# Two matmuls of one weight block joined into one of 512 columns, in the feed-forwards of a two-block transformer kernel

## The chip, the cores and the metric

The kernel runs on one core of a Trainium2 chip. Its time is device microseconds from start to end of one execution. A run of the profiler also gives a span, from the first to the last instruction. The engines are named as in the profile: PE is the matrix engine and PEld its weight loads, DVE is VectorE, ACT is ScalarE, POOL is GpSimd, SP issues the transfers.

## The reference

One sequence of 256 tokens with 1024 features goes through two stacks of two layers each. The parts that matter here are the feed-forwards:

```
# first stack, i = 0, 1 (w_ff_in: 1024 x 4096, w_ff_out: 4096 x 1024)
u = rms_norm(h, g_ffn_pre[i])
f = square(relu(u @ w_ff_in[i])) @ w_ff_out[i]
h = h + rms_norm(f, g_ffn_post[i])

# second stack (w_up: 1024 x 5632, w_down: 2816 x 1024); a = h @ w_up
g, u = a[..., :2816], a[..., 2816:]
acc = conv_b + gp[:, 0:T] * conv_w[0] + gp[:, 1:T+1] * conv_w[1] + gp[:, 2:T+2] * conv_w[2]
return (silu(acc) * u) @ w_down        # gp: g padded by one token at both ends
```

The second stack has a main stream of 256 tokens, which goes through the conv feed-forward in both layers, and a context stream of 256 tokens, which goes through it in the first layer only. The rest is attention of four kinds (stick-breaking, dilated, latent with pooling, grouped), gates, norms, and a conditioning product that gives scales and shifts. Everything is float32.

## The kernel before

**Exact sums of two parts.** A float32 number is held as a high part, rounded to the matrix engine's float32r, and a low part, the rest. A product of two such numbers takes three matmuls (`mm3`, L193 to L196): high by high, high by low, low by high. Weights come from memory as float32 blocks of 128 x 1024 into a ring of four buffers (`ws`); ACT casts each block to its high part (L182) and DVE subtracts (L183), in halves of 512 columns, into rings of four high and four low blocks (`wh`, `wl`). The ring buffer is free again when both halves are subtracted.

**Activations.** `Feat` holds the normalised activations with features on partitions, as chunks of 128 features x 256 tokens, each with a high and a low part. A norm (`norm_one`, L241) runs for each half of the tokens: the row's scale from ACT, DVE and POOL, then for every group of chunks one DVE operation that normalises (L251, or L253 with a shift), transposes on PE into a PSUM bank (L230), a copy of the high part by ACT (L199) and a subtraction by DVE (L200). A group is four chunks (512 columns), or two where `paired` is set; with `paired` the high and low parts of a pair of chunks are in one tile. Main activations come from a pool of eight 4 KB tiles (`m4`), the context's from one of eleven (`c4`).

**First feed-forward** (`ffn1`, L605). Sixteen groups of 256 hidden features per layer. For a group, `up` takes two blocks of weights; for each of two chunks of 128 hidden features the weight block is the stationary side, and 256 tokens of activations move past it, eight blocks of the 1024 inputs, three matmuls each. Both chunks fill one PSUM bank of 512 columns. Then ReLU (ACT, L622), square (DVE, L623), split. `down` multiplies the hidden features (stationary) by 512 columns of the second matrix, into two accumulators. The loop issues `up` of the next group, a piece of filler work, then `down` of this one.

**Conv feed-forward** (`ffn2`, L1088; `up_chunk`, L1072; `conv_chunk`, L1057). For each of 22 chunks the gate half and the up half are each eight blocks of three matmuls, and fill the two halves of one bank. `conv_chunk` reads them there: a tap with bias on ACT (L1062), two more taps on DVE (L1064, L1066), SiLU (ACT, L1068), a product (DVE, L1069), a split. The context stream runs the same two functions from `ctx_gen`, in groups of four chunks.

**Order.** The engines' programs are laid out by a scheduler at build time from the order of the code and the dependencies, so an engine's order can differ from the code's; at run time each engine goes through its own list in order. The code itself mixes streams: `fill` steps generators of filler work (the context stream, or the conditioning product, whose step loads two 512 KB blocks and multiplies them at L465) by a table of credits, `FILL`, between pieces of the main stream.

**Banks.** PSUM has two accumulators of two banks, two banks for the main stream (`mm`), and two for fillers (`fx`, the conditioning product among them).

Of the kernel before, what the change touches and what calls it, by code (L numbers as in the profile page):

```python
# [9 lines left out]
F32 = mybir.dt.float32  # L10
# [10 lines left out]
T = 256  # L21
# [80 lines left out]
def two_block_kernel(ctx: ExitStack, tc: tile.TileContext, a: dict, out: bass.AP, dbg=None):  # L102
# [20 lines left out]
    def mm1():  # L123
        return mmp.tile([128, 512], F32, tag="mm", name="mm")
# [42 lines left out]
    # ---------------------------------------------------------------- helpers  # L167
# [25 lines left out]
    def mm3(o, lh, ll, rh, rl, start, stop):  # L193
        pe.matmul(o, lh, rh, start=start, stop=False)  # L194
        pe.matmul(o, lh, rl, start=False, stop=False)  # L195
        pe.matmul(o, ll, rh, start=False, stop=stop)  # L196

# [60 lines left out]
    class Feat:  # L258
        """Feature-major activations as an exact sum of two float32r parts, by chunks of 128 features."""

        def __init__(self, alloc, n, name, paired=False):
            self.H, self.L, self.groups = [], [], []
            per = 2 if paired else 4
            for c0 in range(0, n, per):
                cn = min(per, n - c0)
                if paired:
                    t = alloc([128, 2, cn, T], F32R, name)
                    th, tl = t[:, 0], t[:, 1]
                else:
                    th = alloc([128, cn, T], F32R, name + "h")  # L270
                    tl = alloc([128, cn, T], F32R, name + "l")
                self.groups.append((th, tl))
                for c in range(cn):
                    self.H.append(th[:, c, :])
                    self.L.append(tl[:, c, :])

# [9 lines left out]
    def tok_blocks(y, us, blocks, first, last):  # L286
        # y[tt] += us[k]^T @ blocks[k], token tile by token tile
        for tt in range(2):
            ts = slice(tt * 128, (tt + 1) * 128)
            for k, ((uh, ul), (bh, bl)) in enumerate(zip(us, blocks)):  # L290
                for nh in range(2):
                    s = slice(nh * 512, nh * 512 + 512)
                    mm3(y[tt][:, s], uh[:, ts], ul[:, ts], bh[:, 0, s], bl[:, 0, s],
                        first and k == 0, last and k == len(us) - 1)
# [13 lines left out]
    # ---------------------------------------------------------------- fillers  # L308
# [40 lines left out]
    def until_dense(n):  # L349
        # bring the context stream to products that wait for nothing  # L350
        clean("mod")
        while queues["ctx"] and dense[0] < n:
            fill_step("ctx")
        credit["ctx"] = 0.0
# [7 lines left out]
    # ------------------------------------------------------------ small setup  # L362
# [17 lines left out]
    def setup_cond():  # L380
        # silu of the two conditionings as columns
        cr = tmp((128, 128))
        nc.sync.dma_start(out=cr[0:8, :], in_=a["c_2"].rearrange("b (k p) -> (b k) p", p=128))
        nc.sync.dma_start(out=cr[8:16, :], in_=a["c_ctx_2"].rearrange("(k p) -> k p", p=128))
        ps = fx1()
        pe.transpose(ps[:, 0:16], cr[0:16, :], ident[0:16, 0:16])
        gp.memset(cst, 0.0)
        act.activation(out=cst[:, :, 0:2], in_=ps[:, 0:16].rearrange("p (r k) -> p k r", r=2), func=AF.Silu)

    def setup_later():  # L390
        nc.sync.dma_start(out=misc, in_=ca[:, C_IF:C_END])
        # rope of the first block
# [26 lines left out]
    def setup_last():  # L419
# [6 lines left out]
        # per-feature columns: conv taps and biases, pool scales  # L426
# [21 lines left out]
    # ------------------------------------------------------- conditioning GEMV  # L448
# [27 lines left out]
    # ------------------------------------------------------------ first block  # L476
# [128 lines left out]
    def ffn1(i, u, before_end):  # L605
        w1, w2 = a["w_ff_in"][i], a["w_ff_out"][i]
        G = FF1 // 256
        with tc.tile_pool(name="ff", bufs=2) as p:
# [3 lines left out]
            def up(g):  # L612
                blocks = [wblock(w1, b * 4, 4, g * 256, 256) for b in range(2)]
                ps = mm1()
                for c in range(2):
                    for kc in range(8):
                        bh, bl = blocks[kc // 4]
                        s = slice(c * 128, (c + 1) * 128)
                        mm3(ps[:, c * 256:(c + 1) * 256], bh[:, kc % 4, s], bl[:, kc % 4, s],
                            u.H[kc], u.L[kc], kc == 0, kc == 7)  # L620
                r = p.tile([128, 512], F32, tag="r", name="r")
                act.activation(out=r, in_=ps, func=AF.Relu)  # L622
                vec.tensor_mul(out=r, in0=r, in1=r)  # L623
                hh = p.tile([128, 2, T], F32R, tag="hh", name="hh")
                hl = p.tile([128, 2, T], F32R, tag="hl", name="hl")
                put_split(hh, hl, r.rearrange("p (c t) -> p c t", c=2))
                hT[g] = (hh, hl)
# [190 lines left out]
    # ----------------------------------------------------------- second block  # L818
# [49 lines left out]
    def mla_gen(u, rope, p, alloc, bank, pair, score_pair, res, prev):  # L868
        # queries, keys, values and pooled features of one stream; attends prev keys and its own
# [57 lines left out]
        # keys come out by features: pairs of heads, then the shared rotated part under each head  # L927
# [32 lines left out]
        # pooled features  # L960
# [27 lines left out]
        # attention  # L988
# [9 lines left out]
    def soft_heads(nh, nk, q, k, v, dv, scale, dst, p, al, bank, score_pair):  # L998
        # softmax attention over nk groups of 256 keys; scores of one head run ahead of the transposes of the last
# [57 lines left out]
    def conv_chunk(i, f, ps, p, hh, hl):  # L1057
        # ps: [128, 512] with the gate half and the up half of feature chunk f
        g, u = ps[:, 0:256], ps[:, 256:512]
        cw = cvw[i]  # L1060
        t = p.tile([128, T], F32, tag="cv", name="cv", bufs=2)
        act.activation(out=t, in_=g, func=AF.Identity, scale=cw[:, NCH + f:NCH + f + 1],  # L1062
                       bias=cw[:, 3 * NCH + f:3 * NCH + f + 1])
        vec.scalar_tensor_tensor(out=t[:, 1:T], in0=g[:, 0:T - 1], scalar=cw[:, f:f + 1], in1=t[:, 1:T],  # L1064
                                 op0=ALU.mult, op1=ALU.add)
        vec.scalar_tensor_tensor(out=t[:, 0:T - 1], in0=g[:, 1:T], scalar=cw[:, 2 * NCH + f:2 * NCH + f + 1],  # L1066
                                 in1=t[:, 0:T - 1], op0=ALU.mult, op1=ALU.add)
        act.activation(out=t, in_=t, func=AF.Silu)  # L1068
        vec.tensor_mul(out=t, in0=u, in1=t)  # L1069
        put_split(hh, hl, t)  # L1070

    def up_chunk(i, f, u, bank):  # L1072
        w = a["ffn_w_up_2"][i].rearrange("k (r n) -> k r n", r=2)
        ps = bank()
# [5 lines left out]
        for r in range(2):  # L1080
            for kc in range(8):
                bh, bl = blocks[kc // 4]
                o = (kc % 4) * 256 + r * 128
                mm3(ps[:, r * 256:(r + 1) * 256], bh[:, o:o + 128], bl[:, o:o + 128], u.H[kc], u.L[kc],
                    kc == 0, kc == 7)
# [49 lines left out]
    def ctx_norm(k, i, m):  # L1135
        g, sft = mod_row(i, 1, m + 1), mod_row(i, 1, m)
        u = Feat(c4, KC, "uc")
# [71 lines left out]
    def gain_tables(p, grow):  # L1209
        # per token and feature: gain x cos, and the gain of the partner feature x (-sin, +sin)  # L1210
# [18 lines left out]
    def gain_rope(x, ps, nh, tt, tables):  # L1229
        # x = rotated gain * ps for token-major heads of 128  # L1230
# [112 lines left out]
    # ------------------------------------------------------------------ order  # L1343
    def main_norm(g, shift=None):
        u = Feat(m4, KC, "u")
# [105 lines left out]
```

## Time and profile before

| | |
|---|---|
| median of three runs | 1740.43 us (1735.95, 1740.43, 1746.13) |
| profiled execution: span | 1732.4 us, 28608 instructions |
| profiled execution: its whole time | not recorded; the timed runs lie 3.6 to 13.7 us above the span |
| mean granted TensorE clock | 0.993 |
| transfers | 337.72 MB, mean 195 GB/s |

A line of the profile names the source line, the engine, the operation, what it writes and reads, and the count; "busy" is the time in which the engine had an instruction in flight, and the mean duration of a matmul includes its pipeline, so that the durations of matmuls overlap. "Idle ... <-" names what ended an engine's idle time. A stretch is given in microseconds from the start of the span. The stick-breaking attention and its projections fill the span up to 195 us, the first feed-forward runs from about 205 to 413, the gate and the dilated attention follow, the second layer's feed-forward runs from 705 to 893, the latent attention from about 950 to 1165, then come the main stream's conv feed-forward (1180 to 1405), the grouped attention, and the last conv feed-forward (1534 to 1717).

### The profile page before, as it was taken

What the parts mean: (1) busy time and instruction counts of PE and PEld (TensorE: products, weight loads), DVE (VectorE), ACT (ScalarE), POOL (GpSimd) and SP (SyncE); (2) the same over time, 40 slices, a digit from 0 to 9 for tenths busy, and PEclk for the clock granted to TensorE, in tenths of its full rate; (3) what the DMA queues carried; (4) which work ended last, traced back from release to release, by engine and by line L of the source; (5) the groups of instructions that cost most, each with busy time, mean ns of one, the idle gap of its engine ahead of it and who ended that gap; (6) DMA issues with size and microseconds to landing.
All of it is one profiled execution on the core that took longest, in us unless ns stands there. A gap on an engine that the chain in (4) does not pass through costs nothing.

```text
span 1732.4 us, 28608 instructions
## 1 busy us (share of the span) xinstructions
PE 1662.8 (96%) x10465; PEld 1428.1 (82%) x10468; DVE 1106.5 (64%) x2153; ACT 925.7 (53%) x1853; POOL 42.3 (2%) x65
## 2 busy tenths in 40 slices
PE   7998999999999999999999999999999999989997
PEld 6767888987887667888888988988999987779997
DVE  4437644557775446744667777767666887766665
ACT  5536544556654435544556556755555555545554
POOL 0000000000000000000000000000000000000000
PEclk9999999999999999999999999999999999989999
DMA  7777577654666666676756655446666765246663
GB/s 237 259 260 250 178 243 260 215 182 142 212 193 211 206 193 206 198 255 231 226 173 191 201 164 166 131 146 202 188 204 188 244 197 169 67 153 186 186 187 99
DMA packets 301073, 337.72 MB, mean 195 GB/s; under 512 B 18400, under 2 KB 246180, under 8 KB 300932
## 3 DMA queue, kind: packets, MB, share of 16 engines
q1 hardware_dynamic: 300932, 335.89, 61.7%
q8 instruction: 82, 1.34, 0.3%
q14 instruction: 59, 0.48, 0.1%
HBM read 332.57 MB, written 3.24 MB: 194 GB/s over the span
## 4 chain that ended last, share of the span: by engine, by line
PE 45%; DMA 5%; DVE 5%; ACT 2%; issue 1%; POOL 1%; SPq 0%; POOLq 0%; ACTq 0%; DVEq 0%
PE mm L196 6%; PE mm L194 6%; PE mm L195 6%; PE acc L195 5%; PE acc L196 5%; PE acc L194 5%; PE fx L196 3%; PE fx L194 3%; PE fx L195 3%; DMA ws<-in_w_ff_out 2%; DMA ws<-in_w_ff_in 2%; DVE wl L183 2%; PE acc L1007 1%; ACT wh L182 1%; PE mm L1033 1%
## 5 line engine op out<-in xcount | busy, mean ns | idle before, releaser
L183 DVE TENSOR_TENSOR wl<-ws,wh 128x512 fp32r<-128x512 f32 x1004 | 638.9, 668 | 402.7 <-ACT wh L182 391.4
L182 ACT CAST wh<-ws 128x512 fp32r<-128x512 f32 x1004 | 567.4, 603 | 510.3 <-PE mm L195 125.2
L194 PE MATMUL mm<-uh,wh 128*128 128x256 f32 x1344 | 382.8, 285 | 2.9 <-ACT wh L182 2.2
L196 PE MATMUL mm<-uh,wl 128*128 128x256 f32 x1344 | 382.0, 284 | 0.9 <-DVE wl L183 0.9
L195 PE MATMUL mm<-ul,wh 128*128 128x256 f32 x1344 | 381.6, 284 | 0.0
L194 PEld LDWEIGHTS mm<-uh,wh 128*128 128x128 f32 x1344 | 258.7, 192 | 8.7 <-ACT wh L182 3.0
L195 PEld LDWEIGHTS mm<-ul,wh 128*128 128x128 f32 x1344 | 258.8, 193 | 3.0 <-issue 0.4
L196 PEld LDWEIGHTS mm<-uh,wl 128*128 128x128 f32 x1344 | 258.7, 192 | 2.1 <-DVE wl L183 1.9
L194 PE MATMUL acc<-wh,hh 128*128 128x512 f32 x432 | 172.1, 398 | 0.0
L196 PE MATMUL acc<-wh,hl 128*128 128x512 f32 x432 | 169.6, 393 | 0.0
L195 PE MATMUL acc<-wl,hh 128*128 128x512 f32 x432 | 169.2, 392 | 0.0
L194 PEld LDWEIGHTS acc<-wh,hh 128*128 128x128 f32 x432 | 81.3, 188 | 28.7 <-ACT wh L182 5.9
L196 PE MATMUL fx<-uch,wl 128*128 128x256 f32 x352 | 100.6, 286 | 2.9 <-DVE wl L183 2.8
L194 PE MATMUL fx<-uch,wh 128*128 128x256 f32 x352 | 101.0, 287 | 1.7 <-DVE fsum L1191 1.7
L195 PE MATMUL fx<-ucl,wh 128*128 128x256 f32 x352 | 100.4, 285 | 0.0
L196 PEld LDWEIGHTS acc<-wh,hl 128*128 128x128 f32 x432 | 81.2, 188 | 18.3 <-issue 0.8
L195 PEld LDWEIGHTS acc<-wl,hh 128*128 128x128 f32 x432 | 81.4, 188 | 14.8 <-issue 0.4
L194 PE MATMUL mm<-wh,uh 128*128 128x384 f32 (+1 forms) x256 | 86.0, 337 | 2.1 <-ACT wh L182 1.6
L195 PE MATMUL mm<-wl,uh 128*128 128x384 f32 (+1 forms) x256 | 83.3, 325 | 0.6 <-DVE wl L183 0.6
L196 PE MATMUL mm<-wh,ul 128*128 128x384 f32 (+1 forms) x256 | 82.9, 324 | 0.0
L216 POOL TENSOR_TENSOR s<-s,neghalf 128x1 f32<-128x1 f32 (+2 forms) x52 | 38.7, 744 | 1556.5 <-DVE s L214 1556.5
L465 PE MATMUL fx<-ws,cst 128*32 128x512 f32 x384 | 65.0, 607 | 6.7 <-DMA ws<-in_w_mod 5.7
(397 smaller groups left out, 2658.9 us busy)
## 6 DMA issues: line engine op xcount, KB each, us to landing
ws<-in_ffn_w_up SPq DMA_DIRECT2D x528, 128.0 KB
ws<-in_w_mod SPq DMA_DIRECT2D x96, 512.0 KB
ws<-in_ffn_w_down SPq DMA_DIRECT2D x66, 512.0 KB
ws<-in_w_ff_in SPq DMA_DIRECT2D x64, 512.0 KB
ws<-in_w_ff_out SPq DMA_DIRECT2D x64, 512.0 KB
ws<-in_w_in_dil SPq DMA_DIRECT2D x96, 192.0 KB
ws<-in_w_in_sb SPq DMA_DIRECT2D x24, 512.0 KB
row<-mod SPq DMA_DIRECT2D x19, 512.0 KB
```

Of the source, the lines that this page charges most:

```text
L182: act.copy(out=h[:, s], in_=st[:, s])
L183: vec.tensor_sub(out=l[:, s], in0=st[:, s], in1=f32(h[:, s]))
L194: pe.matmul(o, lh, rh, start=start, stop=False)
L195: pe.matmul(o, lh, rl, start=False, stop=False)
L196: pe.matmul(o, ll, rh, start=False, stop=stop)
L216: gp.tensor_tensor(out=r, in0=v, in1=neghalf.to_broadcast([128, w]), op=ALU.pow)
L465: pe.matmul(ps[32 * q:32 * q + 32, :], cst[:, kc, :], st[:, q2 * 512:(q2 + 1) * 512], start=kc == 0, stop=kc == 7)
L1007: pe.matmul(sc[qt][:, n * 256:(n + 1) * 256], q(hd, qt), k(hd, n), start=True, stop=True)
L1033: pe.matmul(o, v(hd, n, kt), PTs[hd][:, 2 * n + kt, :], start=n == 0 and kt == 0, stop=n == nk - 1 and kt == 1)
```

## The change

`mm_wide` replaces `mm3` in the first matrices of the feed-forwards: the high part of the weight block is loaded once and meets 512 columns, the 256 tokens' high parts and then their low parts; the block's low part meets the high parts alone, in the first 256 columns. A bank so holds one chunk, with two partial sums. `add_halves` copies the second half out with ACT, into a tile that shares the one buffer of the norms' scratch (`junk`), and adds with DVE. To have high and low parts in one tile, the activations of all main norms and of the context's norms are `paired`.

In `ffn1` each chunk of 128 has its own bank, addition, ReLU and square (one DVE operation) and split. In the conv feed-forward the gate half and the up half each have their own bank; the gate is summed into a tile of the pool `xd` (two buffers, shared with the conditioning product's bias and a context tile), the up half into the same tile after the taps have read it.

```diff
+    def mm_wide(o, wh, wl, u, k, start, stop):
+
+        pe.matmul(o, wh, u.HL[k], start=start, stop=False)
+        pe.matmul(o[:, 0:256], wl, u.H[k], start=False, stop=stop)
+
+    def add_halves(out, ps):
+        b = tmpp.tile([128, 512], F32, tag="junk", name="hb", bufs=1)[:, 0:256]
+        act.copy(out=b, in_=ps[:, 256:512])
+        vec.tensor_tensor(out=out, in0=ps[:, 0:256], in1=b, op=ALU.add)
...
+                if paired:
+                    self.HL.append(t[:, :, c, :])
...
             def up(g):
                 blocks = [wblock(w1, b * 4, 4, g * 256, 256) for b in range(2)]
-                ps = mm1()
+                hh = p.tile([128, 2, T], F32R, tag="hh", name="hh")
+                hl = p.tile([128, 2, T], F32R, tag="hl", name="hl")
                 for c in range(2):
+                    ps = mm1()
                     for kc in range(8):
                         bh, bl = blocks[kc // 4]
                         s = slice(c * 128, (c + 1) * 128)
-                        mm3(ps[:, c * 256:(c + 1) * 256], bh[:, kc % 4, s], bl[:, kc % 4, s],
-                            u.H[kc], u.L[kc], kc == 0, kc == 7)
-                r = p.tile([128, 512], F32, tag="r", name="r")
-                act.activation(out=r, in_=ps, func=AF.Relu)
-                vec.tensor_mul(out=r, in0=r, in1=r)
-                hh = p.tile([128, 2, T], F32R, tag="hh", name="hh")
-                hl = p.tile([128, 2, T], F32R, tag="hl", name="hl")
-                put_split(hh, hl, r.rearrange("p (c t) -> p c t", c=2))
+                        mm_wide(ps, bh[:, kc % 4, s], bl[:, kc % 4, s], u, kc, kc == 0, kc == 7)
+                    r = p.tile([128, 256], F32, tag="r", name="r")
+                    add_halves(r, ps)
+                    vec.scalar_tensor_tensor(out=r, in0=r, scalar=0.0, in1=r, op0=ALU.max, op1=ALU.mult)
+                    put_split(hh[:, c, :], hl[:, c, :], r)
...
     def conv_chunk(i, f, ps, p, hh, hl):
-        # ps: [128, 512] with the gate half and the up half of feature chunk f
-        g, u = ps[:, 0:256], ps[:, 256:512]
         cw = cvw[i]
+        g = fillp.tile([128, 512], F32, tag="xd", name="cg", bufs=2)[:, 0:T]
+        add_halves(g, ps[0])
...
+        add_halves(g, ps[1])
         act.activation(out=t, in_=t, func=AF.Silu)
-        vec.tensor_mul(out=t, in0=u, in1=t)
+        vec.tensor_mul(out=t, in0=g, in1=t)
...
     def up_chunk(i, f, u, bank):
         w = a["ffn_w_up_2"][i].rearrange("k (r n) -> k r n", r=2)
-        ps = bank()
+        ps = [bank(), bank()]
...
-                mm3(ps[:, r * 256:(r + 1) * 256], bh[:, o:o + 128], bl[:, o:o + 128], u.H[kc], u.L[kc],
-                    kc == 0, kc == 7)
+                mm_wide(ps[r], bh[:, o:o + 128], bl[:, o:o + 128], u, kc, kc == 0, kc == 7)
...
     def ctx_norm(k, i, m):
-        u = Feat(c4, KC, "uc")
+        u = Feat(c4, KC, "uc", paired=True)
...
     def main_norm(g, shift=None):
-        u = Feat(m4, KC, "u")
+        u = Feat(m4, KC, "u", paired=True)
```

## Rows read from the trace of the kernel before

**Rows 1.** The page's first part: busy us, share of the span, instructions.
```profile
PE 1662.8 (96%) x10465; PEld 1428.1 (82%) x10468; DVE 1106.5 (64%) x2153; ACT 925.7 (53%) x1853; POOL 42.3 (2%) x65
```

**Rows 2.** The page's fourth part: shares of the chain that ended last, by engine.
```profile
PE 45%; DMA 5%; DVE 5%; ACT 2%; issue 1%; POOL 1%; SPq 0%; POOLq 0%; ACTq 0%; DVEq 0%
```

**Rows 3.** Stretches: busy us (count) by engine, then PE clock, DMA share, GB/s.
```profile
734.00:824.00 90.00, 88.62 (x569) 73.55 (x561) 43.07 (x68) 38.07 (x69) 0.00 (x0) 1.00 0.70 238
836.00:892.00 56.00, 56.00 (x362) 51.20 (x361) 32.17 (x51) 28.13 (x51) 0.00 (x0) 1.00 0.68 215
...
1185.00:1360.00 175.00, 175.00 (x1223) 164.34 (x1223) 120.64 (x218) 93.48 (x186) 0.00 (x0) 1.00 0.67 202
1540.00:1715.00 175.00, 175.00 (x1250) 165.45 (x1249) 112.80 (x209) 94.97 (x189) 0.00 (x0) 1.00 0.58 175
```

**Rows 4.** Groups on PE, 734 to 824: count, busy us, mean ns, idle.
```profile
L465 PE MATMUL fx<-ws,cst 128*32 128x512 f32 x64 | 8.5, 605 | 0.0
```

**Rows 5.** The chain of waits in order of time: start us, us, what.
```profile
723.11 4.52 DMA ws<-in_w_ff_out
727.73 0.63 ACT wh L182
728.39 1.31 DVE wl L183 x2
729.71 3.88 DMA ws<-in_w_ff_in
```

**Rows 6.** Timeline of PE, 836.4 to 847.8: start us, us, instruction, count.
```profile
836.47 0.40 PE L194 MATMUL acc<-wh,hh 128*128 128x512 f32 x1
...
841.71 0.39 PE L196 MATMUL acc<-wh,hl 128*128 128x512 f32 x1
841.93 0.28 PE L194 MATMUL mm<-uh,wh 128*128 128x256 f32 x1
...
847.69 0.40 PE L194 MATMUL acc<-wh,hh 128*128 128x512 f32 x1
```

**Rows 7.** Groups by line and shape, whole run: the blocks' first products.
```profile
L194 PE MATMUL mm<-uh,wh 128*128 128x256 f32 x1344 | 382.8, 285 | 2.9 <-ACT wh L182 2.2 <-DVE ul L200 0.5
...
L194 PE MATMUL fx<-uch,wh 128*128 128x256 f32 x352 | 101.0, 287 | 1.7 <-DVE fsum L1191 1.7
```

**Rows 8.** The same view, operations like the added and removed ones.
```profile
L200 DVE TENSOR_TENSOR hl<-r,hh 128x512 fp32r<-128x512 f32 x32 | 22.0, 687 | 0.8
L623 DVE TENSOR_TENSOR r<-r 128x512 f32<-128x512 f32 x32 | 21.9, 685 | 3.8 <-ACT r L622 3.7
...
L622 ACT ACTIVATE r<-mm 128x512 f32<-128x512 f32 x32 | 19.0, 593 | 4.9 <-PE mm L196 4.9
...
L1064 DVE SCALAR_TENSOR_TENSOR cv<-mm,cvw,cv 128x255 f32<-128x255 f32 x44 | 21.0, 477 | 0.6 <-ACT cv L1062 0.4
...
L1069 DVE TENSOR_TENSOR cv<-mm,cv 128x256 f32<-128x256 f32 x44 | 18.7, 424 | 21.2 <-ACT cv L1068 21.2
...
L200 DVE TENSOR_TENSOR hl<-cv,hh 128x256 fp32r<-128x256 f32 x44 | 18.4, 419 | 2.8 <-ACT hh L199 2.8
...
L717 ACT COPY tok<-mm 128x256 f32<-128x256 f32 x24 | 8.9, 371 | 8.1 <-PE mm L196 8.0
```

**Rows 9.** Waits from 734 to 824: total us, times, longest us.
```profile
PEld acc L194 <- ACT r L622: 2.5, 3, 0.8
```

**Rows 10.** Timeline of the norm at 1527, its end, with the first product.
```profile
1531.31 0.74 DVE L253 SCALAR_TENSOR_TENSOR t<-t,s,row 128x512 f32<-128x512 f32 x1
...
1531.97 0.68 DVE L200 TENSOR_TENSOR ul<-mm,uh 128x512 fp32r<-128x512 f32 x1
...
1532.57 0.68 DVE L183 TENSOR_TENSOR wl<-ws,wh 128x512 fp32r<-128x512 f32 x1
...
1533.97 0.58 PE L194 MATMUL mm<-uh,wh 128*128 128x256 f32 x1
```

**Rows 11.** What PE waited for before the flips (L230): total us, times.
```profile
  DVE t L251: 20.3, 7
```

More of the change, by code (lines that the diff above doesn't have):

```diff
@@ L261, in __init__ @@
         def __init__(self, alloc, n, name, paired=False):
-            self.H, self.L, self.groups = [], [], []
+            self.H, self.L, self.HL, self.groups = [], [], [], []
             per = 2 if paired else 4
```

## The prediction

> **What bounds the kernel now.** I read the busy shares first: TensorE's matmuls cover 96% of the 1732.4 us span, VectorE 64%, ScalarE 53% [rows 1]. The reader should see one engine that is nearly full and two that are not. The chain of waits says the same less strongly: PE has 45% of it, DMA and DVE 5% each [rows 2]. Next, stretch by stretch. From 1185 to 1360 and from 1540 to 1715 (the two conv feed-forwards of the main stream) PE is busy for all 175 us of 175, and also for all 56 us of 836 to 892, the end of the second layer's first feed-forward [rows 3]. There every matmul nanosecond removed is a nanosecond of the span, as long as the other engines keep up: VectorE stands at 120.6 and 112.8 us of 175. The stretch 734 to 824 differs: PE idles 1.4 of 90 us, and the transfers run at 238 GB/s. There eight loop turns each take a step of the conditioning product as well, with two more 512 KB loads (64 records of L465: a step has four products, and each is recorded twice) [rows 4], and the chain of waits runs through DMA, cast, subtraction and the next DMA, round and round, with no matmul in it [rows 5]: the ring of four weight buffers is as late as PE.
>
> **What a matmul costs.** A matmul's duration column is a pipelined latency and can't be summed; I take start to start. Forty-eight 256-column matmuls follow each other from 841.93 to 847.69: 120.0 ns each. The twenty-four 512-column ones before them run from 836.47 to 841.93: 227.5 ns each [rows 6]. So 512 columns cost less than twice 256: 240 against 227.5, a fixed part of some 12.5 ns per matmul. That difference is what the change sells.
>
> The Trainium skill (TensorE: Matmul & The Clock Gate, "Back-to-back issue gap") puts the gap at the columns over 2.4 GHz plus about 2.5 ns. By that rule each fusion saves 2.5 ns, 3.9 us over 1568 of them. The rows contradict it: 120.0 and 227.5 ns leave 12.5 ns at stake, not 2.5.
>
> **Removed.** Every block had three 256-column matmuls, 360 ns; now one of 512 and one of 256, 347.5 ns. The blocks: 32 groups x 16 = 512 in the first block's feed-forwards, 44 chunks x 16 = 704 in the main conv feed-forwards, 22 x 16 = 352 in the context stream's. The first two and 128 blocks of the stick-breaking projections are the 1344 of "mm", the last the 352 of "fx" [rows 7]. 1568 x 12.5 ns = 19.6 us, 0.2 us for each group or chunk. The new moving operand is two pieces of 256 columns, 512 columns apart; no row has such an operand. I take 227.5 ns; the bounds are 215 (twice the 107.5 ns by which 256 more columns lengthen a matmul, with no fixed part) and 240 (no gain).
>
> What of it reaches the end: the 44 main chunks run where PE is full, 8.8 us; the 16 groups without a conditioning step too, 3.2 us. Of the 16 groups beside a conditioning step (eight per layer: the row of L465 over 215 to 310 reads the same) 3.2 us are at stake, and the buffer ring takes most: I count 1.0, bounds 0 and 3.2. The context chunks, 4.4 us, are fillers, some in stretches where PE has gaps: I count 3.0. Together 16.0 us.
>
> **Added on ScalarE and VectorE.** A copy of the second half out of PSUM is like the 256-wide copy of L717, 371 ns; the addition is like L1069, 424 ns (one operand in PSUM, one not) [rows 8]. Per conv chunk: two copies 0.74 us, two additions 0.85 us. Per group of the first feed-forward: ReLU (593) becomes two copies (742); the 512-wide square (685) and split subtraction (687) become two additions (848), two fused max-multiply (by L1064, 477 each: 954) and two subtractions (2 x 419): VectorE +1.27 us. For 1540 to 1715 that makes some 22 x 0.85 = 19 us more, DVE 131 of about 171; in 1185 to 1360, with some 17 main and four context chunks, 139 of about 171. PE hides it: both still have 20% idle. If that cover went, a microsecond of delay per turn would cost 76 us over 32 groups and 44 chunks.
> The chains behind the products do not get longer: the gate half now has its own bank and is read while the up half multiplies, some 2.8 us earlier (eight blocks of 347.5 ns), and in the first feed-forward the last half is 256 wide. In 734 to 824 PE's weight loads waited 2.5 us for that ReLU [rows 9]; some of this may go.
>
> **Added in the banks.** A chunk now holds both banks of its pool. The first bank is freed while the second half multiplies, the second about 371 + 424 ns after the end, in the main loops under a down product of 12 x 227.5 = 2.7 us. Where two chunks stand back to back (each loop's first two, the context groups of four) up to half a microsecond shows: 1.5 us in all, bounds 0 and 6.
>
> **Moved: the norms.** The activations of all ten main norms and three context norms now come in pairs of chunks, so each token half makes four flips of two transposes, not two of four. In the norm at 1527 the normalising operations (L253) and the subtractions follow each other on VectorE 0.66 and 0.60 us apart, and PE waits for them between the transposes [rows 10]; over the run such waits for L251 alone hold back PE for 20.3 us in 7 places [rows 11]. At 256 columns I take the starts 0.40 and 0.345 us apart (477 and 419 ns, less the 75 ns by which a start comes before the end). Eight of each cost 5.96 us against 4 x 1.27 = 5.1: +0.86. The last flip has two transposes fewer: -0.22. That is +0.64 us for a norm that VectorE paces; context matmuls stand between the transposes of several, so I count 0.5 each: 5 us for ten. Bounds -2 (only the shorter tail shows) and +17 (each flip waits for its bank: 1.7 us a norm). SP's queue issues the same DMAs in the same order; POOL gets nothing new.
>
> **Sum.** -16.0 + 5.0 + 1.5 = -9.5 us: the profiled span would go from 1732.4 to about 1723. The whole time of that execution isn't shown; the median of the three runs, 1740.4, lies 8.0 us above its span, and I keep that distance: 1731 us.
>
> **Rivals.**
> Full gain: the norms' longer chain hides behind context matmuls and the shorter ReLU tail gives back what the buffer ring takes. For it: fillers stand at most norms. Against: the waits of rows 11. Time: 1740.4 - 18 = about 1722.
> Eaten up: the flips are paced by their two banks, +1.2 us per norm, and the context chunks' gain is lost in gaps: -13 + 12 + 2 = +1, 1741. Against it: the shorter transposes and copies.
> Slower, from ScalarE's and VectorE's order: their queues run in order, and each half now puts a copy that waits for PE, and an addition behind it, ahead of casts and subtractions of weights already landed. In 734 to 824 the ring has no slack, so 2 x 0.4 us per group over 32 groups would cost 25 us against 16 gained, plus the norms: +14, 1754. It decides once a cast is held up longer than PE's stock of converted blocks lasts (four buffers). For it: the ring's chain passes through a cast and a subtraction at every turn [rows 5]. Against: half of the new work comes earlier than the old.
> The change does not do what it says: the two-piece operand costs two matmuls' 240 ns. Then only the norms and banks stay: 5.0 + 1.5 = +6.5, 1747. For it: no row has such an operand. Against: the 227.5 ns of every 512-column row. The Trainium skill's rule above (same page and section) leads nearly as far, to -3.9 + 6.5, about 1743; the rows of 120.0 and 227.5 ns speak against it.
>
> **How the numbers follow.** Forecast 0.48, full gain 0.17, eaten up 0.16, slower 0.13, no cheaper matmul 0.06. Half a per cent, 8.7 us, is about what a measurement of this kernel can tell from no change; the three runs alone spread over 10 us. The forecast lies at that line: a little over half of it counts as faster. Faster 0.27 + 0.17 = 0.44; same 0.21 + 0.16 + 0.03, half of the last, = 0.40; slower 0.13 + 0.03 = 0.16. The forecast's own range is 1724 to 1738. For 8 in 10 I go down into the full gain, 1718, and up past "eaten up" and the 240 ns matmul to 1749.
>
> **What would show it.** Right: in 1540 to 1715's stage a turn of 8.5 us becomes 8.3, with a 512-column "mm" starting 227 ns before the next matmul; PE full there still. In the turns with a conditioning step nearly the same period as before, the chain still through DMA. In the norms sixteen transposes in eight pairs, and from the first normalising operation to the first product some 0.6 us more. Wrong: a pitch of 240 ns; waits of PE for casts or subtractions in the conv stages; PE held up by the added copy or addition, for a bank; or norms no longer than before, and the time near 1722.

## The result, and the profile after

| | before | after |
|---|---|---|
| median (range, runs) | 1742.59 us (1735.95 to 1746.13, 4) | 1760.99 us (1757.69 to 1771.23, 4) |
| ratio after / before | | 1.012 [1.008, 1.016] |
| profiled execution: span | 1732.4 us | 1756.2 us |
| profiled execution: whole time | not recorded | 1758.04 us |
| mean granted TensorE clock | 0.993 | 0.983 |

The kernel is 1.2% slower; the forecast was 1731 us, with a range of 1718 to 1749. The whole time of an execution turns out to lie 1.8 us above its span, not 8: the profiled execution of before then took 1734 us, less than any of the four runs. So the spans' difference of 23.8 us is some 5 us larger than the medians' of 18.4, and where sizes matter below I use ratios and not spans.

The page's first part after: busy us, share of the span, instructions.
```profile
PE 1666.0 (95%) x8896; PEld 1346.0 (77%) x8900; DVE 1194.1 (68%) x2517; ACT 981.8 (56%) x2100; POOL 41.4 (2%) x65
```
Against [rows 1], 1569 matmuls are gone, yet PE is busy 3.2 us longer and idle 20.6 us longer (1756.2 less 1666.0 is 90.2, before it was 69.6). Both halves need an answer.

The stretches that answer to [rows 3], after: busy us (count) by engine, PE clock, DMA share, GB/s.
```profile
742.00:832.00 90.00, 89.33 (x463) 68.99 (x461) 51.55 (x101) 40.45 (x84) 0.00 (x0) 1.00 0.70 238
845.00:901.00 56.00, 56.00 (x285) 47.44 (x284) 39.34 (x75) 31.71 (x66) 0.00 (x0) 1.00 0.70 214
1200.00:1375.00 175.00, 175.00 (x915) 148.20 (x914) 133.75 (x259) 107.75 (x228) 0.00 (x0) 1.00 0.65 194
1565.00:1735.00 170.00, 170.00 (x899) 145.10 (x898) 125.13 (x247) 106.85 (x226) 0.00 (x0) 1.00 0.61 180
```
Inside the loops PE is full as forecast, VectorE and ScalarE have room for the copies and additions, and from 742 to 832 transfers run at 238 GB/s as before. The loss is elsewhere. PE's longest waits after, and what it waited for (us, times, longest):
```profile
PE mm L240 <- DVE t L261: 17.1, 4, 9.9
PE mm L240 <- DVE t L263: 12.3, 2, 6.1
...
PE mm L200 <- DVE cg L206: 4.4, 1, 4.4
```
The same view of before has these (L230, L251 and L253 there are L240, L261 and L263 here):
```profile
PE mm L230 <- DVE t L251: 10.1, 4, 8.8
PE mm L230 <- DVE t L253: 7.4, 3, 6.4
```
So 11.9 us more go into waiting for a norm's first operation, and 4.4 us into one conv chunk's addition. To see why, one norm is followed in both kernels. The timeline of before, PE with one of ACT's squares, at the norm of the second layer's first feed-forward (start us, us, instruction, idle before and releaser):
```profile
693.83 0.39 PE L196 MATMUL acc<-wh,o 128*128 128x512 f32 x1
694.05 0.28 PE L194 MATMUL fx<-uch,wh 128*128 128x256 f32 x1
...
696.36 1.06 ACT L222 ACTIVATE junk<-h 128x1024 bf16<-128x1024 f32 x1
...
700.05 0.28 PE L196 MATMUL fx<-uch,wl 128*128 128x256 f32 x1
700.66 0.66 PE L230 MATMUL mm<-ident,t 128*128 128x128 f32 x4 [0.34 <-DVE t L251]
```
After, the same place, with ACT's squares and the copy:
```profile
687.41 0.28 PE L201 MATMUL fx<-uc,wl 128*128 128x256 f32 x1
...
701.91 0.39 PE L196 MATMUL acc<-wh,o 128*128 128x512 f32 x1
702.40 1.02 ACT L232 ACTIVATE junk<-acc 128x1024 bf16<-128x1024 f32 x1 [0.28 <-PE acc L196]
704.44 1.05 ACT L232 ACTIVATE junk<-h 128x1024 bf16<-128x1024 f32 x1
706.93 1.06 ACT L232 ACTIVATE junk<-h 128x1024 bf16<-128x1024 f32 x1 [1.34 <-DVE s L224]
708.11 0.37 ACT L205 COPY hb<-fx 128x256 f32<-128x256 f32 x1
708.48 0.93 PE L240 MATMUL mm<-ident,t 128*128 128x128 f32 x3 [6.18 <-DVE t L261]
...
713.49 0.41 DVE L206 TENSOR_TENSOR cg<-fx,hb 128x256 f32<-128x256 f32 x1
714.04 0.77 PE L200 MATMUL fx<-uc,wh 128*128 128x512 f32 x1
```
Before, six microseconds of a context chunk's products run from 694.05 to 700.05, while ACT squares the main stream for its norm (L222); PE has a gap of 0.34 us. After, a context chunk's sixteen blocks are done at 687.7 and hold both `fx` banks. Their first copy, L205, of the gate half, comes out at 708.11, behind all the squares (L232): both write the one `junk` buffer. Its addition (L206) starts at 713.49, behind the norm's own work on VectorE, and only then, at 714.04, does the next context product start. PE has nothing to put beside the norm, and stands for 6.18 us.

The gap has a second part. Stretches after, around the waits before the norms of 708 and 1186 and a third one, told below:
```profile
706.00:716.00 10.00, 6.28 (x21) 3.74 (x22) 8.76 (x22) 4.98 (x13) 1.41 (x2) 0.50 0.45 152
1184.00:1194.00 10.00, 6.71 (x22) 4.17 (x23) 8.95 (x22) 5.10 (x13) 1.36 (x2) 0.50 0.49 166
1392.10:1398.80 6.70, 4.96 (x17) 3.80 (x18) 6.03 (x15) 3.76 (x11) 0.55 (x1) 0.50 0.78 241
```
The granted clock falls to 0.50, its 1.2 GHz level, within each of these waits and is still there when PE goes on (at 714.04 the 512-column product takes 0.77 us, elsewhere 0.40); before, 699 to 709 reads 1.00. Over all stretches recorded at 0.50, first in before, then in after, the sums are (length in us, then each engine's busy us in them):
```profile
sum 25.30, PE 14.85 PEld 11.10 DVE 12.96 ACT 5.87 POOL 1.72; mean PE 3.71 PEld 2.77 DVE 3.24 ACT 1.47 POOL 0.43
sum 60.20, PE 42.08 PEld 29.73 DVE 41.77 ACT 22.07 POOL 5.03; mean PE 5.26 PEld 3.72 DVE 5.22 ACT 2.76 POOL 0.63
```
If half of PE's busy time in them is lost, that is 7.4 us before and 21.0 after. By this estimate the spans' 23.8 us are 20.6 of idle time and 13.6 of half clock, less 10.4 of work that is gone: that is why PE's busy time grew although its matmuls became fewer. Part of the 13.6 is luck of one execution: the profiled one of before has a mean clock of 0.993, while the median over the runs of before beside the experiments is 0.986 to 0.988, and over the four runs of after 0.9805.

The third place is a main chunk. After, 1388 to 1395, PE, ACT and DVE:
```profile
1388.95 0.39 PE L196 MATMUL acc<-wh,hl 128*128 128x512 f32 x1
1391.68 1.06 ACT L232 ACTIVATE junk<-xc 128x1024 bf16<-128x1024 f32 x1 [1.12 <-DMA xc<-xc]
1392.86 0.37 ACT L205 COPY hb<-mm 128x256 f32<-128x256 f32 x1
1393.26 0.42 DVE L206 TENSOR_TENSOR cg<-mm,hb 128x256 f32<-128x256 f32 x1 [0.25 <-ACT hb L205]
1393.74 0.80 PE L200 MATMUL mm<-u,wh 128*128 128x512 f32 x1 [4.41 <-DVE cg L206]
```
Here the copy stands behind the square of a context norm, which waits for its transfer of `xc`. By way of a scratch buffer, a bank of the main stream waits for a context row to arrive from memory.

The joined matmuls themselves, in the feed-forward's turn that answers to [rows 6], after, PE:
```profile
855.51 0.39 PE L200 MATMUL mm<-u,wh 128*128 128x512 f32 x1
855.74 0.28 PE L201 MATMUL mm<-u,wl 128*128 128x256 f32 x1
855.85 0.40 PE L200 MATMUL mm<-u,wh 128*128 128x512 f32 x1
...
861.04 0.28 PE L201 MATMUL mm<-u,wl 128*128 128x256 f32 x1
861.15 0.40 PE L194 MATMUL acc<-wh,hh 128*128 128x512 f32 x1
```
Sixteen blocks take 5.64 us, 352.5 ns each, where 48 matmuls took 5.76, 360 each. Over the loops the starts lie 235.8 ns apart after a wide and 116.9 after a narrow one: 352.7 in all, so 7.3 ns are won per block, not 12.5. A turn of the last conv loop takes 8.39 us, before 8.50; the forecast was 8.3.

### The profile page after: what moved, and what is told of

Read it like the earlier page. It is cut to its first block, busy times and chain, and to the rows that moved or that the text cites. A ratio compares the mean times of both kernels' runs of the same rounds, so it can differ in the third digit from the quotient of the medians.

```text
span 1756.2 us, 26252 instructions
## 1 busy us (share of the span) xinstructions
PE 1666.0 (95%) x8896; PEld 1346.0 (77%) x8900; DVE 1194.1 (68%) x2517; ACT 981.8 (56%) x2100; POOL 41.4 (2%) x65
## 4 chain that ended last, share of the span: by engine, by line
PE 70%; DMA 13%; DVE 9%; ACT 4%; issue 2%; POOL 1%; SPq 1%; ACTq 0%; POOLq 0%; DVEq 0%
PE mm L200 12%; PE acc L195 6%; PE acc L196 6%; PE acc L194 6%; PE mm L201 6%; DMA ws<-in_w_ff_out 5%; PE fx L200 4%; DVE wl L183 4%; DMA ws<-in_w_ff_in 3%; PE mm L194 3%; PE mm L195 3%; PE mm L196 3%; PE fx L194 3%; PE fx L195 2%; PE fx L196 2%; PE fx L201 2%
## 5 line engine op out<-in xcount | busy, mean ns | idle before, releaser
L200 PE MATMUL mm<-u,wh 128*128 128x512 f32 x1216 | 436.1, 400 | 9.2 <-ACT wh L182 4.7
L201 PE MATMUL mm<-u,wl 128*128 128x256 f32 x1216 | 343.5, 283 | 1.9 <-DVE wl L183 1.8
L200 PEld LDWEIGHTS mm<-u,wh 128*128 128x128 f32 x1216 | 229.6, 189 | 66.5 <-ACT wh L182 7.1
L201 PEld LDWEIGHTS mm<-u,wl 128*128 128x128 f32 x1216 | 230.7, 190 | 8.0 <-DVE wl L183 5.0
L200 PE MATMUL fx<-uc,wh 128*128 128x512 f32 x352 | 130.0, 409 | 2.2 <-DVE fsum L1203 2.2
L205 ACT COPY hb<-mm 128x256 f32<-128x256 f32 x152 | 56.0, 368 | 84.3 <-PE mm L201 80.4
L201 PE MATMUL fx<-uc,wl 128*128 128x256 f32 x352 | 101.4, 289 | 0.0
L194 PE MATMUL mm<-wh,u 128*128 128x384 f32 (+1 forms) x256 | 86.9, 342 | 2.2 <-ACT wh L182 1.3
L195 PE MATMUL mm<-wl,u 128*128 128x384 f32 (+1 forms) x256 | 84.6, 330 | 0.7 <-DVE wl L183 0.6
L196 PE MATMUL mm<-wh,u 128*128 128x384 f32 (+1 forms) x256 | 84.1, 329 | 0.0
L200 PEld LDWEIGHTS fx<-uc,wh 128*128 128x128 f32 x352 | 67.9, 193 | 19.7 <-DVE fsum L1203 2.3
L240 PE MATMUL mm<-ident,t 128*128 128x128 f32 x170 | 40.5, 345 | 37.8 <-DVE t L261 17.1
L201 PEld LDWEIGHTS fx<-uc,wl 128*128 128x128 f32 x352 | 68.2, 194 | 1.2 <-issue 0.7
```

Of the source, the lines that this page charges most:

```text
L200: pe.matmul(o, wh, u.HL[k], start=start, stop=False)
L201: pe.matmul(o[:, 0:256], wl, u.H[k], start=False, stop=stop)
L205: act.copy(out=b, in_=ps[:, 256:512])
L240: pe.transpose(ps[:, j * 128:(j + 1) * 128], src[:, j * 128:(j + 1) * 128], ident)
```

## Experiments

Each was timed beside the kernel before, whose median there is 1742.6 to 1744.3 us. A ratio stands with its 95% interval in brackets, and need not be the quotient of the medians (e6: 0.9941, by the medians 0.992). The theory after the result, with the letters that the expectations use: the shared scratch buffer costs the time (J). Rivals: a context chunk now takes both filler banks, so that the next cannot start (B); the operand in two pieces (P); the paired norms (N); the copies and additions as such (called D here).

**e1: a place of its own for the copy.** The kernel after; the second half goes to the unused half of the sum's own tile.
```diff
-    def add_halves(out, ps):
-        b = tmpp.tile([128, 512], F32, tag="junk", name="hb", bufs=1)[:, 0:256]
+    def add_halves(out, ps, b):
...
-                    r = p.tile([128, 256], F32, tag="r", name="r")
-                    add_halves(r, ps)
+                    r2 = p.tile([128, 512], F32, tag="r", name="r")
+                    r = r2[:, 0:256]
+                    add_halves(r, ps, r2[:, 256:512])
...
-        add_halves(g, ps[0])
+        add_halves(g, ps[0], g2[:, T:2 * T])
```


> The changed kernel, but the copy of a bank's second half goes to the unused half of the tile that takes the sum, no longer to the norms' one scratch buffer. Theory J (shared scratch: the copy waits behind a norm's squares, the bank stays taken, PE waits): the PE waits of 6.5 us before the norms at 708 and 1186 and of 4.8 us at 1389 of the changed kernel go, with the half-clock stretches behind them, and the time falls by 12 to 18 us to about 1745. Theory B (a context chunk takes both filler banks, so the next cannot start under a norm): those waits stay, at most 5 us come back, 1756 or more.

Measured 1741.11 us, ratio 0.9997 [0.9975, 1.0019]. The buffer's sharing is worth 1.2%, 21 us, and without it no effect of the change on the time can be told from zero. A context chunk still takes both banks here, so B does not explain the loss. PE at the norm shown above, in e1, with the copy (L204):
```profile
699.21 0.39 PE L196 MATMUL acc<-wh,o 128*128 128x512 f32 x1
699.43 0.39 PE L200 MATMUL fx<-uc,wh 128*128 128x512 f32 x1
...
702.79 0.36 ACT L204 COPY cg<-fx 128x256 f32<-128x256 f32 x1
...
705.08 0.40 PE L200 MATMUL fx<-uc,wh 128*128 128x512 f32 x1
705.46 0.83 PE L239 MATMUL mm<-ident,t 128*128 128x128 f32 x4
```
The context's products are back beside the norm, with no wait, and the first half's copy starts 0.4 us after the end of its product, between two of the norm's squares. PE's idle time is 76.4 us (1736.8 less 1660.4), against 90.2.

**e2: the wide operand in one piece.** The kernel after, with high and low parts of a chunk side by side.
```diff
-                    t = alloc([128, 2, cn, T], F32R, name)
-                    th, tl = t[:, 0], t[:, 1]
+                    t = alloc([128, cn, 2, T], F32R, name)
+                    th, tl = t[:, :, 0, :], t[:, :, 1, :]
...
-                        self.HL.append(t[:, :, c, :])
+                        self.HL.append(t[:, c, :, :].rearrange("p two t -> p (two t)"))
```


> The changed kernel, but the high and low parts of one chunk lie side by side, so the 512 moving columns are one piece. Theory P (the wide matmul costs 236 ns on the mean instead of 227 because its operand has two pieces): the pitch of the wide matmul becomes 227 ns, a turn of the last conv feed-forward 8.25 us instead of 8.39, and 8 to 12 us come back, about 1751. Rival (the 236 ns come with the change between a 512 and a 256 column matmul): pitch and time stay, 1761.

Measured 1761.17 us, 1.0105 [1.0076, 1.0134], as the kernel after. PE in its last feed-forward:
```profile
1600.28 0.40 PE L200 MATMUL mm<-u,wh 128*128 128x512 f32 x1
1600.51 0.28 PE L201 MATMUL mm<-u,wl 128*128 128x256 f32 x1
1600.62 0.40 PE L200 MATMUL mm<-u,wh 128*128 128x512 f32 x1
```
From 1590 to 1735 the means are the same 235.8 and 116.9 ns, and a turn takes 8.39 us as after. P falls: two pieces cost nothing here, and why 512 columns take 235.8 ns among narrow matmuls and 227.5 among wide ones stays open.

**e3: the pairs alone.** The kernel before, with one line changed in each of two norms.
```diff
-        u = Feat(c4, KC, "uc")
+        u = Feat(c4, KC, "uc", paired=True)
...
-        u = Feat(m4, KC, "u")
+        u = Feat(m4, KC, "u", paired=True)
```


> The kernel before, with nothing changed but the activations of the norms in pairs of chunks (eight flips of two transposes per norm for four of four); all products stay as they were. Theory N (the norms cost most of the loss): 8 to 15 us slower than the kernel before, 1751 to 1757. Theories J and B (the loss lies in the banks and the scratch): at most 6 us slower, 1743 to 1749.

Measured 1758.04 us, 1.008 [1.0053, 1.0107]: 13.9 us slower with no other part of the change. From its first to its last transpose a main norm takes 6.4 us on average instead of 4.9, 15.1 us over the ten. The end of the span's last norm, PE:
```profile
1551.49 1.09 PE L230 MATMUL mm<-ident,t 128*128 128x128 f32 x4 [6.68 <-DVE t L253]
1553.07 0.69 PE L230 MATMUL mm<-ident,t 128*128 128x128 f32 x2 [0.49 <-DVE u L200]
1554.13 1.41 PE L230 MATMUL mm<-ident,t 128*128 128x128 f32 x4 [0.38 <-DVE u L200]
1555.74 1.42 PE L230 MATMUL mm<-ident,t 128*128 128x128 f32 x4 [0.19 <-DVE u L200]
1557.40 0.69 PE L230 MATMUL mm<-ident,t 128*128 128x128 f32 x2 [0.24 <-DVE u L200]
```
Most of these flips wait for the subtraction that frees a bank. Over the whole span, what PE waited for before them (us, times):
```profile
  DVE u L200: 20.7, 40
```
The same line of before reads 11.3 us in 16. So N is true as well, beside J. How the longer norms become time is shown in part only. With the same 10465 matmuls, e3's profiled execution has PE idle for 76.4 us (before 69.6) and busy for 1680.4 (before 1662.8). Its clock is lower, too: the median over e3's runs is 0.9815, over the runs of before beside it 0.986, which is worth at most some 8 of the 13.9 us (an estimate, from the clock's difference times 1744 us). That the 15.1 us come near the 13.9 does therefore not show that each microsecond of a norm comes back as one of time. Pairs at 13.9 and sharing at 21 make more than was lost, so the rest of the change must gain; e5 asks which part.

**e4: the context stream as before.** The kernel after, where the context keeps its three matmuls, one bank a chunk, no copy and no pairs; the main stream still copies through `junk`.
```diff
...
-        ps = [bank(), bank()]
+        ps = bank() if bank is fx1 else [bank(), bank()]
...
-                mm_wide(ps[r], bh[:, o:o + 128], bl[:, o:o + 128], u, kc, kc == 0, kc == 7)
+                if isinstance(ps, list):
+                    mm_wide(ps[r], bh[:, o:o + 128], bl[:, o:o + 128], u, kc, kc == 0, kc == 7)
+                else:
+                    mm3(ps[:, r * 256:(r + 1) * 256], bh[:, o:o + 128], bl[:, o:o + 128], u.H[kc], u.L[kc],
+                        kc == 0, kc == 7)
...
-        u = Feat(c4, KC, "uc", paired=True)
+        u = Feat(c4, KC, "uc")
```


> The changed kernel, but the context stream's chunks keep the form of before: three matmuls of 256 columns, both halves in one filler bank, activations not paired, no copy. Theory B: the fillers run under the norms at 708 and 1186 again, 12 to 18 us come back, about 1745. Theory J: nearly the same here, since the context's copies are what waits for the scratch, but the 4.8 us wait at 1389, where a main chunk's copy waits behind a context norm, stays; 8 to 12 us come back, about 1751.

Measured 1748.28 us, 1.0026 [1.0001, 1.0051]. Three quarters of the loss go with the context's part of the change. The time lies between what J (1751) and B (1745) asked for and does not decide between them; of the three waits above only the one at 1394 is left, with 3.7 us, as J said.

**e5: no joining.** e1, with the wide matmul as two narrow ones into the two halves of the bank; copies, additions, banks and pairs stay.
```diff
-        pe.matmul(o, wh, u.HL[k], start=start, stop=False)
+        pe.matmul(o[:, 0:256], wh, u.H[k], start=start, stop=False)
+        pe.matmul(o[:, 256:512], wh, u.L[k], start=False, stop=False)
```


> The kernel with its own copy buffer (1741 us), but the joined matmul taken apart: three matmuls of 256 columns per block, into the two halves of the bank; pairs, banks, copies and additions stay. The pitches of the changed kernel (235.8 + 116.9 ns against three of 120.0) say that joining is worth 1568 x 7.3 ns = 11.4 us: 1752 us. As predicted before the change, 12.5 ns per block: 1758. If the copies and the two banks cost something as well, that shows in no difference here.

Measured 1749.61 us, 1.0049 [1.0029, 1.0069]. Against e1 the joining is worth 0.52%, 9.0 us; 1568 times 7.3 ns are 11.4. Against e3 the copies, additions and second banks come to -0.31%, -5.4 us, with intervals that overlap: D falls, as they cost nothing that can be told from zero.

**e6: pairs only where they are used.** e1, with pairs in the four norms ahead of feed-forwards and the context's one, the other norms as before.
```diff
-        u = Feat(c4, KC, "uc", paired=True)
+        u = Feat(c4, KC, "uc", paired=k == 1)
...
-    def main_norm(g, shift=None):
-        u = Feat(m4, KC, "u", paired=True)
+    def main_norm(g, shift=None, paired=False):
+        u = Feat(m4, KC, "u", paired=paired)
...
-        u = main_norm(row(a["g_ffn_pre"][i]))
+        u = main_norm(row(a["g_ffn_pre"][i]), paired=True)
...
-        u = main_norm(mod_row(i, 0, 4), mod_row(i, 0, 3))
+        u = main_norm(mod_row(i, 0, 4), mod_row(i, 0, 3), paired=True)
```


> The kernel with its own copy buffer (1741 us), but only the norms in front of the feed-forwards (four main ones and one of the context) in pairs of chunks; the other eight keep groups of four. Theory N (the pairs cost 14 us over thirteen norms, about one each): 8 us come back, 1733. Rival (the pairs cost where the filler work is displaced in the feed-forwards, not in each norm): within 3 us of 1741.

Measured 1728.19 us, 0.9941 [0.9915, 0.9966], faster than both kernels. Against e1 that is 0.56%, 9.8 us, for six main norms and two of the context's; by e3's 13.9 us for thirteen norms, eight are worth 8.6.

**e7: flips of four again.** e6, with a norm that normalises and transposes four chunks at a time into one bank; only the copies and subtractions stay by pairs.
```diff
-            flip_group(u[:, s], grp, tt, bank)
-            c0 += w
+            ps = bank()
+            for j in range(4):
+                pe.transpose(ps[:, j * 128:(j + 1) * 128], u[:, c0 + j * 128:c0 + (j + 1) * 128], ident)
...
+                put_split(th[:, :, ts], tl[:, :, ts], pv[:, j:j + per, :])
```


> As the run with pairs in front of the feed-forwards alone, but the norm works on four chunks at a time there as well: one normalising operation of 512, four transposes into one bank, then two copies and two subtractions of 256. If the number of normalising operations and flips matters, 2 to 4 us less than that run, about 1730; if only the number of copies and subtractions matters, the same as that run.

Measured 1729.46 us, 0.9928 [0.9903, 0.9953], no different from e6. The four norms take 4.7 to 6.3 us, hardly less than e6's 5.6 to 6.2 (one of them, at 4.7, is as short as before), so for the other three the number of flips and of normalising operations is not the main thing that lengthens them. What e7 leaves doubled are the copies and subtractions; that these alone do it was not tried by itself.

**e8: e6 with the context as before.** e6, with e4's edit on the context stream.
```diff
-        ps = [bank(), bank()]
+        ps = bank() if bank is fx1 else [bank(), bank()]
...
-        u = Feat(c4, KC, "uc", paired=k == 1)
+        u = Feat(c4, KC, "uc", paired=False)
```


> Own copy buffer, pairs in front of the four main feed-forwards alone, and the context stream as in the kernel before (three matmuls of 256, one filler bank per chunk, no pairs). Theory B (two filler banks per context chunk hold the fillers up even with the copy's own buffer): faster than the run with pairs in front of all five feed-forwards, by 3 us or more. Rival: the context's joined matmuls are worth their 352 x 7.3 ns = 2.6 us, and this run is that much slower.

Measured 1739.36 us, 0.9991 [0.9971, 1.0011]: 0.50%, 8.7 us, above e6, where B asked for 3 us or more below it. With the copy in its own place, two filler banks per context chunk do no harm that shows, and B falls. The 352 joined blocks of the context account for 352 times 7.3 ns, 2.6 us; the rest is not explained.

**e9 and e10: whose copies.** The kernel after, with a place of its own for the context's copies alone (e9), or for the main stream's alone (e10, where the condition below asks for `True`). The lines are told against e1.
```diff
+    def add_halves(out, ps, b, ctx=False):
+        if ctx == False:
+            b = tmpp.tile([128, 512], F32, tag="junk", name="hb", bufs=1)[:, 0:256]
...
+        add_halves(g, ps[0], g2[:, T:2 * T], p is fillp)
```


> The changed kernel with an own copy buffer for the context stream's chunks alone; the main stream's copies still share the norms' scratch. If the context's copies make most of the loss (the waits of 6.2 and 6.1 us before the norms at 708 and 1186), two thirds of the 20 us come back, about 1748, and the wait near 1390 stays. Rival (the main stream's copies make it): 3 to 6 us, about 1757.

> The other way round: own copy buffer for the main stream's chunks, the context's copies share the scratch. If the context's copies make most of the loss: the waits before the norms at 708 and 1186 stay, the one near 1390 goes, 5 to 8 us come back, about 1755. Rival: about 1746.

Measured: e9 1745.42 us, 1.0008 [0.999, 1.0026]; e10 1754.39 us, 1.0073 [1.0045, 1.0102]. PE's waits in e9:
```profile
PE mm L241 <- DVE t L264: 6.7, 1, 6.7
...
PE mm L200 <- DVE cg L207: 4.2, 1, 4.2
```
and in e10:
```profile
PE mm L241 <- DVE t L262: 17.4, 4, 10.3
PE mm L241 <- DVE t L264: 12.8, 2, 6.7
```
With the context's copies out of `junk`, the waits at the norms of 708 and 1186 go and the main chunk's stays (the 6.7 us are at the last norm, where before has 6.4). With the main stream's out it is the reverse: no wait for `cg` is left, and those for the norms' first operation are as after. The context's own place gives back 1.12 of the 1.23 points between the kernel after and e1. The main stream's gives 0.47, with an interval that meets that of the kernel after; the two shares make more than the whole, so they don't simply add.

**e11: another order.** e6 with one credit of filler work changed, to see what a mere shift of the order does.
```diff
-f1c=5.04,
+f1c=5.3,
```


> A control: the kernel with own copy buffers and pairs in front of the feed-forwards alone (1728), with one number of the filler table changed, the credit per group of the first feed-forward from 5.04 to 5.3. No theory gives it a cost; it shows how much a mere shift of the order moves the time. If such shifts move it by 2 us at most, 1726 to 1731, the 8 to 11 us by which the narrow context stream was slower have a cause of their own; if by 5 us or more, they may be such a shift.

Measured 1734.17 us, 0.9943 [0.9921, 0.9966], against e6's 0.9941. So e6's gain holds in a second order as well. For e8 the numbers do not agree: the medians of e11 and e6 are 6.0 us apart, by which the expectation would put e8's difference down to such shifts, and the ratios 0.02%, by which it would have a cause of its own. Some 6 us of it stay open.

## Why the prediction was wrong

The steps in order, each with what the runs put in its place (ratios times 1743 us). The runs' steps lead from before over e3, e5 and e1 to after, so that their sum is the measured one by construction, and is no check on them:

| step | forecast us | runs us |
|---|---|---|
| joining the matmuls (removed) | -16.0 | -9.0 (e1 against e5; by the pitch, -11.4) |
| norms in pairs (moved) | +5.0 | +13.9 (e3) |
| copies, additions, second banks, apart from where the copy lands | +1.5 | -5.4, not told from zero (e5 against e3) |
| the copy's landing place | 0, not seen | +21.4 (after against e1) |
| sum | -9.5 | +20.9 (the ratio 1.012; the medians of the four runs differ by 18.4) |

**The step that failed is "Added in the banks".** It let the second bank come free "about 371 + 424 ns after the end" of the product: it took the price from a copy (L717 in [rows 8]) that waited for PE's product alone, 8.0 of 8.1 us. The price was right, 0.37 us for the copy and 0.41 for the addition. The copy's target was the norms' single scratch buffer, as the diff shows (`tag="junk"`, `bufs=1`). At the norm of 708 the copy starts 20.4 us after the chunk's last product and 26.3 after its own half's, with squares before it in ACT's list that themselves wait for the end of the main stream's products. The cost is not the copy's 0.37 us but the filler work that the two held banks keep out, just where PE needs it, and the half clock behind the gap. The bound of 6 us was drawn from chunks that stand back to back, and did not cover a bank that is held over a norm; of the prediction's own signs of being wrong, "PE held up by the added copy or addition, for a bank" is the one that came.

**"Moved: the norms" was mis-sized by nearly three**: 0.5 us each, against 1.4 in time (13.9 over ten) and 1.5 in length. The rule that VectorE's normalising operations and subtractions pace the norm (+0.64) was too low a limit. The rival "eaten up" was nearer, with flips paced by their two banks at +1.2 per norm: e3's forty waits for the subtraction speak for it. Each pair's bank must go through a copy on ACT and a subtraction on DVE, twice as many of them as with four chunks, and e7, which leaves these alone doubled, can't be told from e6. That context matmuls would leave only 5 us of it was wrong too; how much of the 13.9 is waiting and how much is the lower clock stays open.

**"Removed" was right in kind and too large**, 12.5 ns a block against 7.3. The 12.5 came from rows where all matmuls have one width. Mixed, a block is 352.7 ns. The rival of 240 ns for the wide one was nearer in the single figure (235.8), but the narrow one behind it got cheaper, 116.9 instead of 120.0, and the sum still gains. The gain per block lies between 2.5 ns, the prediction's other figure, and the forecast's 12.5. The Trainium skill (TensorE: Matmul & The Clock Gate, "Back-to-back issue gap") gives the rule with the gap of 2.5 ns for an isolated matmul, and says that weight loads change the spacing in a stream; an estimate by the rule is 215.8 and 109.2 ns, and the trace, with a weight load at each matmul, has more in both places, 235.8 and 116.9.

**"Added on ScalarE and VectorE" was right**: the conv stretches are full, with DVE at 133.8 of 175 and 125.1 of 170 us. The rival that let the copies hold up the casts did not come: from 742 to 832 PE is busy for 89.3 of 90 us, and e5 against e3 gives copies and additions no cost that can be told from zero. The casts there wait for transfers, and PE's weight loads wait for casts little longer than before, where they read 2.5 us in 3 times (us, times, longest):
```profile
ACT wh L182 <- DMA ws<-in_w_ff_out: 24.2, 12, 5.3
...
PEld acc L194 <- ACT wh L182: 3.4, 4, 0.8
```
It had the sign and nearly the time of the result (1754), by a mechanism that isn't there. It asked what stands behind a copy in ACT's list; the answer was in what stands before it.

## What to carry to other kernels

An added copy can cost what its target makes it wait for, and not only what it takes: look up the buffer it writes, who else writes it, and whether a stream that is waiting for something else stands between. Where filler work covers the gaps of a main stream, the fillers' banks are part of that cover, and whatever holds them over a norm costs the norm. And change a layout only for the users that need it: pairs in the norms ahead of the feed-forwards alone, with a place of its own for the copy, turn 1.2% slower into 0.6% faster (e6).

## What the runs showed of the hardware

- Matmuls of float32r with a weight load each: 120.0 ns from start to start where all have 256 columns, 227.5 where all have 512, but 235.8 after the wide and 116.9 after the narrow where they take turns. A moving operand in two pieces or in one makes no difference (e2).
- A gap of PE can be paid more than once. Within the gaps of 4.41, 6.18 and 6.15 us in the kernel after, the granted clock fell from 1.00 to 0.50, and it stayed there for some 7 to 10 us, into the work behind the gap. Over the twelve runs of e1 the time was higher by about 1.4 us for each 0.001 by which the mean granted clock was lower (correlation -0.82; over 23 runs of before 1.3 us, -0.55); that is a correlation, and no run sets the clock by itself.
